# Host-laid parameters and gate weights, smaller first loads, gates one unit later, deferred rows of w_out, and a last product by token tiles

## The chip, the cores and the metric

One core of a Trainium2 chip runs the kernel. TensorE (PE) multiplies matrices, VectorE (DVE) and ScalarE (ACT) work on elements, GpSimd (POOL) does little here, and SyncE's queue (SP) issues DMA transfers. The metric is the device time of one execution in microseconds.

## The reference

One decoder layer for 2048 tokens of width 1024 in fp32:

```python
h = rmsnorm(x, norm_mix_g)
u = h @ w_in                       # 1024 x 3584, split into gate_b, gate_c, v, x_r, g
y_conv = gate_b * causal_dwconv(gate_c * v, conv_w)          # width 512, 3 taps
xr = causal_dwconv(x_r, rnn_conv_w) + rnn_conv_b             # width 1024, 4 taps
r = sigmoid(block_diag(xr, w_a) + b_a); i = sigmoid(block_diag(xr, w_x) + b_x)
a = exp(-8 * r * softplus(-lam)); bx = sqrt(1 - a*a) * (i * xr)
y_rnn = scan(a, bx) * gelu(g)
x = x + concat[rmsnorm(y_conv), rmsnorm(y_rnn)] @ w_out      # 1536 x 1024
h = rmsnorm(x, norm_mlp_g)
x = x + square(relu(h @ w_mlp_in)) @ w_mlp_out               # 1024 x 4096 x 1024
out = rmsnorm(x, final_norm_g)
```

## The kernel before

The tokens are cut into four blocks `b` of 512, and a block into four token tiles `t` of 128. Each fp32 operand is split into a rounded high part and the rest (`hi`, `lo`, type fp32r), and a product is the sum of three passes, hi·hi, lo·hi and hi·lo. ScalarE casts the high parts (line 174), VectorE subtracts for the low parts (line 175).

**Mixers.** `mixers(b, h)` goes through 14 units of 256 columns of `w_in` in the order x0 g0 x1 c0 g1 x2 v0 g2 x3 b0 g3 c1 v1 b1. Each unit is 48 products into one of four PSUM pairs. An x unit goes through `lru_conv` (empties PSUM, four taps on VectorE), `lru_split`, and then `lru_gates`, 12 small block-diagonal products per two column groups with sigmoids on ScalarE; `lru_scan` runs the recurrence on VectorE. Units c, v and b make the short convolution (`conv_c`, `conv_v`, `conv_b`). `part(n)` does pieces of the next block's row norm.

**Block 0's beginning** is written out by hand for ScalarE, VectorE and TensorE. The products of x0 and g0 (`start_x`, `start_g`) start from unnormalised x, loaded transposed; the row factors are computed beside them, spread over the partitions with a product of a diagonal matrix with ones (`spread`, `bc`, line 421) and kept in `row0`, by which VectorE multiplies each of block 0's units when it empties PSUM. The gain `norm_mix_g` and all small parameter vectors are loaded as rows and turned with transposes on TensorE. Two groups of small products with ones (`WARM`) run while the first loads are under way.

**Output projection.** `w_out_rows` multiplies the recurrent half in four row groups `pr` by four token tiles into `po[0..3]`, all four PSUM pairs at once; the fourth pair first serves the next block's spread and the sums for the norm (`stats`). `w_out_conv` adds the convolution's half, and the residual is kept.

**MLP.** Two blocks together form 2x2 block products with seven multiplications instead of eight (the `Up` and `Down` classes; ORDER is 1, 2, 6, 5, 7, 3, 4). In `Down`, product `i` is done in two halves `a`, each over four token tiles; after `a == 1`, `drain` adds PSUM to the residual. In the last quarter of the inner width product 3 completes block b and product 4 completes block b+1 in its first 512 columns. `finish(b)` squares, sums, takes the root, scales and stores each token tile.

Outside the hand-written stretches a scheduler orders each engine's instructions by the place in the program and its own model of time. Weights live in 15 slots (`wp`), other temporaries in 29 (`tp`); `take(name, ahead)` uses a unit's weights, loads those of later units and splits them.

Of the kernel before, what the change touches and what calls it, by code (L numbers as in the profile page):

```python
# [38 lines left out]
def KEEP(u, n):  # L39
# [3 lines left out]
ROWS = [  # L43
    ("conv_w", 12),
# [12 lines left out]
def block_kernel(  # L57
# [3 lines left out]
    norm_mix_g,  # L61
    w_in,
    conv_w,
    rnn_conv_w,
    rnn_conv_b,
    w_a,
    b_a,
    w_x,
    b_x,
    lru_lambda,  # L70
    g_norm_conv,
    g_norm_rnn,
# [5 lines left out]
    x_t,  # L78
    out,
# [184 lines left out]
    ones = cp.tile([P, P], F32, name="ones")  # L264
    nc.gpsimd.memset(ones, 1.0)
# [36 lines left out]
    def load_gates():  # L302

        r = temp("gate_raw", (P, NLRU, P))
        for e in range(2):
            for g, src in enumerate((w_a, w_x)):
                col = 64 * ((g + e) % 2)
                sv = src[0].rearrange("(c e) i j -> e i c j", e=2)
                nc.sync.dma_start(r[64 * e : 64 * e + 64, :, col : col + 64], sv[e])
        return r  # L310
# [9 lines left out]
    g_row = temp("g_row", (KD, P))  # L320

    def start_w(u, i):
# [3 lines left out]
    nc.sync.dma_start(g_row, norm_mix_g[0].rearrange("(k p) -> k p", p=P))  # L326
    load_xt(0, (0,))
    start_w(0, 0)
    load_xt(0, (1,))
    start_w(0, 1)  # L330
    load_xt(0, (2,))
    load_xt(0, (3,))
# [4 lines left out]
    nc.scalar.activation(warm, ones[:, 0:1], AF.Sqrt)  # L337
    nrows = sum(n for _, n in ROWS)
    prow = temp("prow", (P, P))
    srcs = dict(  # L340
        conv_w=conv_w[0].rearrange("k (c q) -> (k c) q", q=P),
        rnn_conv_w=rnn_conv_w[0].rearrange("k (c q) -> (k c) q", q=P),
        rnn_conv_b=rnn_conv_b.rearrange("o (c q) -> (o c) q", q=P),
        b_a=b_a.rearrange("o (c q) -> (o c) q", q=P),
        b_x=b_x.rearrange("o (c q) -> (o c) q", q=P),
        lru_lambda=lru_lambda.rearrange("o (c q) -> (o c) q", q=P),
        g_norm_conv=g_norm_conv.rearrange("o (c q) -> (o c) q", q=P),
        g_norm_rnn=g_norm_rnn.rearrange("o (c q) -> (o c) q", q=P),
    )
    off = {}  # L350
    o = 0
    for nm, n in ROWS:
        if nm == "b_x_swapped":
            for e in range(2):
                nc.sync.dma_start(
                    prow[o : o + n, 64 * e : 64 * e + 64],
                    srcs["b_x"][:, 64 - 64 * e : 128 - 64 * e],
                )
# [713 lines left out]
    def w_out_rows(b, ysB, accB, during):  # L1072
        po = [psum("po") for _ in range(NT)]
        for pr in range(4):
# [4 lines left out]
            if pr:  # L1079
                during(pr)  # L1080
# [263 lines left out]
```

## Time and profile before

| | us |
|---|---|
| median of three runs | 2173.37 (2171.5 to 2177.3) |
| profiled execution, own time | 2173.16 |
| its span, first to last instruction | 2171.4 |
| TensorE busy | 2152.1 |
| VectorE busy | 1471.3 |
| ScalarE busy | 983.1 |

The span is what the trace covers; the profiled execution's own time is 1.76 us more. The engines work side by side, so their busy times don't add up. A line such as `PE po L421 <- DVE u L730: 3.3, 1, 3.3` says that TensorE, at line 421, stood idle 3.3 us in total until VectorE's line 730 was done, once, and at longest 3.3 us. In a timeline a row begins with its start and its duration in us. In a table of windows, the columns behind the stretch are its length, the busy time and number of instructions of PE, PEld, DVE, ACT and POOL, the granted TensorE clock, the DMA share and GB/s.

### The profile page before, as it was taken

What the parts mean: (1) busy time and instruction counts of PE and PEld (TensorE: products, weight loads), DVE (VectorE), ACT (ScalarE), POOL (GpSimd) and SP (SyncE); (2) the same over time, 40 slices, a digit from 0 to 9 for tenths busy, and PEclk for the clock granted to TensorE, in tenths of its full rate; (3) what the DMA queues carried; (4) which work ended last, traced back from release to release, by engine and by line L of the source; (5) the groups of instructions that cost most, each with busy time, mean ns of one, the idle gap of its engine ahead of it and who ended that gap; (6) DMA issues with size and microseconds to landing.
All of it is one profiled execution on the core that took longest, in us unless ns stands there. A gap on an engine that the chain in (4) does not pass through costs nothing.

```text
span 2171.4 us, 25196 instructions
## 1 busy us (share of the span) xinstructions
PE 2152.1 (99%) x9634; PEld 1773.1 (82%) x9634; DVE 1471.3 (68%) x1763; ACT 983.1 (45%) x1300; POOL 43.5 (2%) x50
## 2 busy tenths in 40 slices
PE   9999999999999999999999999999999999999997
PEld 7887888888888888888888888888888888888886
DVE  6878636668666678778754653545886666887866
ACT  6784355436533343334445623562464333333343
POOL 0100000000000000000001000000000000000000
PEclk9999999999999999999999999999999999999999
DMA  7898875742453576444285657456335355854422
GB/s 266 301 334 289 332 281 194 277 140 93 154 189 117 184 305 247 152 153 153 103 313 203 244 211 271 177 197 247 107 125 195 117 187 201 328 175 155 136 97 78
DMA packets 177769, 435.82 MB, mean 201 GB/s; under 512 B 17809, under 2 KB 68081, under 8 KB 177649
## 3 DMA queue, kind: packets, MB, share of 16 engines
q1 hardware_dynamic: 177648, 434.22, 54.8%
q8 instruction: 76, 1.25, 0.2%
q14 instruction: 45, 0.36, 0.0%
HBM read 312.53 MB, written 121.63 MB: 200 GB/s over the span
## 4 chain that ended last, share of the span: by engine, by line
PE 91%; DVE 4%; DMA 2%; ACT 2%; issue 1%; SPq 0%; POOL 0%; DVEq 0%; ACTq 0%; POOLq 0%
PE up L811 28%; PE dn L929 27%; PE po L253 12%; PE ps_x L229 6%; PE ps_g L229 6%; PE ps_c L229 3%; PE ps_v L229 3%; PE ps_b L229 3%; PE psri L652 1%; DVE xr L617 1%; DMA raw<-in_w_in_dram 1%; PE tps L1098 1%; PE start_x L488 1%; DMA xT<-in_x_t_dram 1%; DVE x L973 0%
## 5 line engine op out<-in xcount | busy, mean ns | idle before, releaser
L811 PE MATMUL up<-H,w_hi 128*128 128x512 f32 x1792 | 552.1, 389 | 0.0
L811 PEld LDWEIGHTS up<-H,w_hi 128*128 128x128 f32 x1792 | 336.0, 188 | 69.7
L811 PE MATMUL up<-H,w_lo 128*128 128x512 f32 x896 | 348.6, 389 | 0.0
L929 PE MATMUL dn<-w_hi,z_hi 128*128 128x512 f32 x896 | 348.5, 389 | 0.0
L929 PE MATMUL dn<-w_lo,z_hi 128*128 128x512 f32 x896 | 348.5, 389 | 0.0
L929 PE MATMUL dn<-w_hi,z_lo 128*128 128x512 f32 x896 | 348.5, 389 | 0.0
L175 DVE TENSOR_TENSOR w_lo<-w,w_hi 128x1024 fp32r<-128x1024 f32 x156 | 190.7, 1223 | 129.0 <-PE dn L929 51.3
L174 ACT CAST z_hi<-z 128x1024 fp32r<-128x1024 f32 x112 | 118.2, 1056 | 353.2 <-PE dn L929 314.2
L174 ACT CAST w_hi<-w 128x1024 fp32r<-128x1024 f32 x156 | 163.8, 1050 | 250.0 <-PE up L811 123.3
L929 PEld LDWEIGHTS dn<-w_hi,z_lo 128*128 128x128 f32 x896 | 168.2, 188 | 35.1
L929 PEld LDWEIGHTS dn<-w_hi,z_hi 128*128 128x128 f32 x896 | 168.2, 188 | 34.9
L929 PEld LDWEIGHTS dn<-w_lo,z_hi 128*128 128x128 f32 x896 | 168.2, 188 | 34.8
L811 PEld LDWEIGHTS up<-H,w_lo 128*128 128x128 f32 x896 | 168.2, 188 | 34.8
L941 DVE TENSOR_TENSOR x<-dn,x 128x1024 f32<-128x1024 f32 x112 | 136.8, 1221 | 24.9 <-PE dn L929 23.5
L175 DVE TENSOR_TENSOR z_lo<-z,z_hi 128x1024 fp32r<-128x1024 f32 x112 | 136.6, 1219 | 15.1 <-ACT z_hi L174 15.1
L253 PE MATMUL po<-w_hi,y_hi 128*128 128x512 f32 x384 | 121.1, 397 | 0.0
L253 PE MATMUL po<-w_lo,y_hi 128*128 128x512 f32 x384 | 119.0, 390 | 0.0
L253 PE MATMUL po<-w_hi,y_lo 128*128 128x512 f32 x384 | 118.7, 390 | 0.0
L608 DVE TENSOR_SCALAR xr<-xr_in,prm 128x512 f32<-128x512 f32 x32 | 17.3, 550 | 115.3 <-ACT xr_in L601 115.2
L229 PE MATMUL ps_x<-h_hi,w_hi 128*128 128x512 f32 x240 | 93.5, 390 | 0.0
L229 PE MATMUL ps_g<-h_hi,w_hi 128*128 128x512 f32 x240 | 93.5, 390 | 0.0
L229 PE MATMUL ps_x<-h_lo,w_hi 128*128 128x512 f32 x240 | 93.4, 389 | 0.0
(234 smaller groups left out, 3469.6 us busy)
## 6 DMA issues: line engine op xcount, KB each, us to landing
w_hi<-d_w SPq DMA_DIRECT2D x114, 512.0 KB
w_lo<-d_w SPq DMA_DIRECT2D x114, 512.0 KB
z<-d_z SPq DMA_DIRECT2D x112, 512.0 KB
w<-in_w_mlp_in_dram SPq DMA_DIRECT2D x64, 512.0 KB
d_z<-snap SPq DMA_DIRECT2D x64, 512.0 KB
d_z<-z SPq DMA_DIRECT2D x48, 512.0 KB
w<-in_w_mlp_out_dram SPq DMA_DIRECT2D x48, 512.0 KB
d_w<-w_hi SPq DMA_DIRECT2D x40, 512.0 KB
```

What stands on the lines that cost most here:

```text
L174: nc.scalar.copy(hi, src)
L175: return (lo_engine or V).tensor_tensor(lo, src, hi.bitcast(F32), SUB).ins
L229: nc.tensor.matmul(ps[:, j, lo:hi], ws[k // 4][:, k % 4, j * P : (j + 1) * P], hs[:, k, lo:hi], start=k == 0 and i == 0, stop=k == KD - 1 ...
L253: nc.tensor.matmul(ps[:, half, :], ys[:, j, t * P : (t + 1) * P], ws[j][:, 0, half * 512 : (half + 1) * 512], start=first and i == 0, stop ...
L488: nc.tensor.matmul(start_x[:, j], w[a][k // 4][:, k % 4, j * P : (j + 1) * P], h[c][:, k], start=k == 0 and n == 0, stop=k == KD - 1 and n ...
L608: V.tensor_scalar(xr[:, j, :], xr_in[:, j, 0:TB], par("rnn_conv_w", c), par("rnn_conv_b", c), MUL, ADD,)
L617: V.scalar_tensor_tensor(xr[:, j, :], xr_in[:, j, k : k + TB], par("rnn_conv_w", 8 * k + c), xr[:, j, :], MUL, ADD,)
L652: nc.tensor.matmul(pr_[:, e, :], ws[own, c, :], xsrc[own, j, :], start=i == 0, stop=i == 2)
L811: nc.tensor.matmul(ps[:, j, :], ws[:, k, j * P : (j + 1) * P], hs(k), start=i in (1, 2, 5) and k == 0 and n == 0, stop=k == 3 and n == len ...
L929: nc.tensor.matmul(ps[t // 2][:, t % 2, :], zs[:, p, t * P : (t + 1) * P], ws[:, p, :], start=i in (1, 2, 5) and a == 0 and p == 0 and n == 0,
L941: V.tensor_add(xt[b, th, dh], ps[th], xt[b, th, dh])
L1098: nc.tensor.transpose(ps[:, k, :], xs[:, k // 4, k % 4 * P : (k % 4 + 1) * P], ident)
```

## The change

1. The host hands over `rows_t` (all parameter vectors, `norm_mix_g` among them, already turned to 128 partitions by 104 columns) and `gate_w` (the gate weights as the kernel keeps them). One transfer each takes the place of 11 row transfers with two transposes, and of four transfers.
2. The first loads are 256 KB instead of 512 KB, and the first two weight pieces are issued on ScalarE's queue. The casts of the first weights go in four pieces too.
3. x1 joins x0 and g0 in the hand-written beginning, and the spread comes in the middle of x1. `spread` becomes two fp32r products (high and low part of the diagonal) instead of one fp32 product. For block 0 the square of the row factor is kept as well, so that `conv_c` multiplies by the square and `conv_v` has one multiplication less; the remaining one moves from `conv_b` to the end of `conv_v`.
4. `lru_conv` is cut into `lru_take` (empties PSUM) and the taps, and each gate stage comes one unit later: behind c0, v0, b0 and c1 instead of x1, x2, x3 and g3. The split of the second y moves from `w_out_rows` to the end of `mixers`.
5. In `w_out_rows` the fourth token tile of row groups 0 and 1 is done after the other three tiles of both; `take` of group 1 looks one unit ahead instead of two.
6. In the last quarter of `Down`, product 4 is done with both halves for one token tile after the other, in the order 0, 2, 1, 3 (`multiply_last`), and each tile is added, squared, scaled and stored at once. The class `Finish` squares the 512 columns that are complete earlier, and multiplies them by the gain, under the products before; ScalarE scales these columns at the end.

```diff
+    nc.sync.dma_start(prm, rows_t)
+    for q in range(4):
+        r = temp("xT")
+        for i in range(2):
+            k0 = 256 * q + 128 * i
+            nc.sync.dma_start(r[:, i, :], x_t[k0 : k0 + P, 0:TB])
...
+        ks = slice(2 * (q % 2), 2 * (q % 2) + 2)
+        (nc.scalar if q < 2 else nc.sync).dma_start(
+            raws[0][q // 2][:, ks, :], units[0][1][0][q // 2][:, ks, :]
+        )
...
     def diagonal(rs, n):
-        diag = temp("diag", (P, n, P))
+        hi = temp("diag_hi", (P, n, P), F32R)
+        lo = temp("diag_lo", (P, n, P), F32R)
         for k in range(n):
-            V.tensor_scalar(diag[:, k, :], ident, rs[:, k : k + 1], None, MUL)
-        return diag
+            f = rs[:, k : k + 1]
+            V.tensor_scalar(hi[:, k, :], ident, f, None, MUL)
+            V.scalar_tensor_tensor(lo[:, k, :], ident, f, hi[:, k, :].bitcast(F32), MUL, SUB)
+        return hi, lo
...
         mm_cols(start_g, w, h, 0, ks=range(4, KD))
+        mm_cols(start_g, w, h, 1, ks=range(4, KD))
+        w = take("x1", ahead=0)
+        start_x1 = psum("start_x1")
+        mm_cols(start_x1, w, h, 0, ks=range(4))
+        mm_cols(start_x1, w, h, 1, ks=range(4))
         bc = spread(diag, NT)
...
+        mm_cols(start_x1, w, h, 0, ks=range(4, KD))
+        mm_cols(start_x1, w, h, 1, ks=range(4, KD))
+        nc.scalar.copy(row0[:, 0], bc)
+        nc.scalar.activation(row0[:, 1], bc, AF.Square)
...
         gs = lru_gelu(0, h, row)
-        psx = col_unit("x1", h)
+        x_in = lru_take(1, col_unit("x1", h), row)
+        gc = conv_c(0, h, row2)
+        part(0)
+        part(1)
         st = lru_gates(0, xr, xs, gs)
-        xr = lru_conv(1, psx, row)
+        xr = lru_conv(1, x_in)
...
+            w = take("oB%d" % pr, ahead=1 if pr == 1 else OUT_AHEAD)
...
             for t in range(NT):
+                if pr < 2 and t == 3:
+                    held.append((y, w))
+                    continue
                 for j in range(2):
                     mm_rows(po[t], y, w, j, t, pr == 0 and j == 0, pr == 3 and j == 1)
+            if pr == 1:
+                if b + 1 < NB:
+                    next_part(b + 1, 8, po[3][:, 0, :])
+                rB = stats(accB, D, "B", po[3][:, 1, 0:NT])
+                for n, (y, w) in enumerate(held):
+                    during(n)
+                    for j in range(2):
+                        mm_rows(po[3], y, w, j, 3, n == 0 and j == 0, False)
...
+            def take_tile(t, ps):
+                self.add(t, ps)
+                if t == 0:
+                    other.factors(0, NT)
+                if t in (0, 2):
+                    other.rows(t, 2)
+                if held:
+                    end(held.pop())
+                held.append(t)
+                if t == NT - 1:
+                    end(held.pop())
...
+                end = s == NS // 2 - 1
+                if not (end and i == 4):
+                    downs[s].multiply(i, a)
+                    if a == 1:
+                        downs[s].drain(i, b)
+                elif a == 1:
+                    downs[s].multiply_last(ends[1].tiles(ends[0]))
...
+                if end and (i, a) == (5, 0):
+                    ends = [Finish(b, 0), Finish(b + 1, 1)]
+                    ends[0].first()
+                if end and (i, a) == (3, 1):
+                    for t in range(NT):
+                        ends[0].add(t, None)
+                if end and (i, a) == (7, 1):
+                    ends[1].first()
```

More of the change, by code (lines that the diff above doesn't have):

```diff
@@ L1061, in mixers @@
         fold(accB)
-        part(3)
-        gc = conv_c(1, h, row)
-        part(4)
+        part(6)
         load_x(b)
```

303 lines of the change are left out of this document (170 added, 133 removed).

## The prediction

> **What bounds the kernel now.** I read the busy times first, then who waited for whom on TensorE, then the chain of waits, then the windows around each place where TensorE stands still.
>
> ```profile
> span 2171.4 us, 25196 instructions
> PE 2152.1 (99%) x9634; PEld 1773.1 (82%) x9634; DVE 1471.3 (68%) x1763; ACT 983.1 (45%) x1300; POOL 43.5 (2%) x50
> PE po L421 <- DVE u L730: 3.3, 1, 3.3
> PE start_x L488 <- ACT w_hi L472: 2.4, 1, 2.4
> 5.89 1.33 ACT h_hi L468 x2
> 7.24 1.05 ACT w_hi L472
> 8.33 12.60 PE start_x L488 x48
> 29.10 0.88 PE bc L421 x2
> 269.16 10.88 PE ps_x L229 x48
> 415.12 0.86 PE po L421 x2
> ```
>
> TensorE is busy 99% of the span. A unit of 48 products takes 10.88 us, 0.227 us each, whether it is x, g, c, v or b. So only three things can shorten this kernel: TensorE idling, TensorE at a lower clock, and products that are not needed. TensorE waits 2.4 us before its first real product and 3.3 us once in the first output projection; the rest of its idle time is the tail behind the last product. Nothing between 190 us and that tail is a stall, so whatever the change does there can only hold or lose.
>
> Everything is counted against the profiled execution: 2173.16 us, 1.76 above its span, and 0.21 below the median of 2173.37.
>
> **The start.** Loads land in the order issued, and a landing is seen about 1.1 us after the bytes have moved.
>
> ```profile
> 0.73 1.28 ACT L337 ACT_TABLE_LOAD   x1 [0.73 <-PEq L1330]
> 2.00:4.75 2.75, 2.75 (x14) 2.50 (x14) 0.17 (x1) 0.40 (x4) 0.00 (x0) 1.00 0.79 189
> 2.00:6.35 4.35, 3.95 (x23) 3.51 (x22) 0.17 (x1) 0.86 (x5) 0.00 (x0) 1.00 0.88 252
> 20.77 0.39 PE L229 MATMUL start_g<-h_hi,w_hi 128*128 128x512 f32 x1
> ```
>
> By 4.75 us 0.52 MB had moved (2.75 us at 189 GB/s): the first 512 KB block of x transposed, used from 5.89. By 6.35 it is 1.1 MB, which brings the first weight block, cast at 7.24. After, the first product wants the parameter table (53 KB), 256 KB of x and 256 KB of weights, 0.57 MB, the weights issued on ScalarE's queue. With two queues sharing the engines, part of the second x piece moves too: some 0.62 MB, there at 5.1 us, seen at 6.2. Then one cast of x (1.33/2 = 0.67) and one of half a weight block (0.53) put the first product at 7.4 instead of 8.33. If ScalarE's transfers stand behind its table load (1.28 us) the weights start later but x alone sooner; the same arithmetic gives 6.9 to 7.4. A quarter of `start_x` needs 1.9 us of ScalarE (two casts of x, one of weights), about 2.1 of VectorE and 12 products x 0.227 = 2.72 of TensorE, so TensorE then sets the pace, with about 0.3 us of waiting in the first quarter.
>
> `start_x` now runs from 8.33 to 20.77, 12.44 us instead of 10.88. The clock says why:
>
> ```profile
> 7.50:8.00 0.50, 0.00 (x0) 0.00 (x0) 0.50 (x1) 0.50 (x1) 0.00 (x0) 0.96 1.02 358
> 8.00:8.50 0.50, 0.17 (x1) 0.17 (x2) 0.25 (x2) 0.28 (x1) 0.00 (x0) 0.50 1.08 383
> 11.00:11.50 0.50, 0.50 (x3) 0.39 (x2) 0.49 (x1) 0.29 (x1) 0.00 (x0) 0.63 1.08 408
> 4.54:7.95 3.41, 1.41 (x12) 1.22 (x11) 1.30 (x2) 2.05 (x3) 0.00 (x0) 1.00 1.03 363
> ```
>
> The granted clock falls to 0.50 near 7.95 us and comes back near 11.3: 3.4 us at half speed, 1.7 us lost. In the 3.41 us before the fall TensorE was busy for 1.41. After, the warm-up products are as many and end at about the same time, 5.9, and the first real product comes 0.9 us earlier, so that stretch would be some 55% busy instead of 41%. The bounds are: clock kept (gain 0.9 + 1.7 - 0.3 = 2.3) and clock lost again (from 7.4 on, ending near 19.9: gain 0.9). The nearest row is the fall itself; I take 0.9. The Trainium skill ("TensorE: Matmul & The Clock Gate", section "The HAM clock gate") has the throttle decided in free-running windows of about 3.4 us, fully throttled after an idle one. The 3.4 us of half speed agree with the length; that a stretch 41% busy was enough to lose the clock is harsher than the page's idle window. By the page's wording a mostly busy window would keep the clock, and the start would gain 2.3.
>
> Behind it, `start_g` to the next unit takes 32.65 - 20.77 = 11.88 us:
>
> ```profile
> 32.65 0.39 PE L229 MATMUL ps_x<-h_hi,w_hi 128*128 128x512 f32 x1
> ```
>
> 1.0 of that is not products of the unit: the fp32 spread of row factors (0.88) and the transpose of the parameters. After, the transpose is gone and the spread is two fp32r products, 0.45. Gain 0.55. The third unit's weights, split in the prologue, cost 2 casts and 2 subtractions (about 1.05 and 1.22 each) on engines that have over 20 us for them.
>
> The same spread stands in three later output projections at 0.86: 3 x (0.86 - 0.45) = 1.2 gained, on TensorE's own path. The extra VectorE instructions for its low part (4 x about 0.25 us per block) lie beside products.
>
> **The stall in the first output projection.** For batch block 0:
>
> ```profile
> 170.45 0.61 PE L253 MATMUL po<-w_hi,y_hi 128*128 128x512 f32 x2
> 182.09 2.07 PE L421 MATMUL po<-diag,ones 128*128 128x512 f32 x2 [3.31 <-DVE u L730]
> 221.14 0.79 PE sps L582 x8
> 406.79 0.62 PE L253 MATMUL po<-w_hi,y_hi 128*128 128x512 f32 x2
> 452.64 0.79 PE sps L582 x8
> 182.00:183.00 1.00, 0.91 (x1) 0.50 (x2) 0.04 (x1) 0.93 (x1) 0.00 (x0) 0.52 0.09 37
> ```
>
> From the stage's first product to the statistics behind it: 50.69 us in block 0, 45.85 in block 1. The difference, 4.8 us, is 3.3 of stall and the rest a half clock after it. TensorE wants the fourth PSUM pair, still held by the last mixer unit until VectorE has multiplied it out (line 730). After, tokens 384 to 511 of the first two row groups come after the rest, so the fourth pair is wanted 36 products = 8.2 us later. Against that, VectorE's whole block-0 work starts later in TensorE's order: the spread comes after 48+48+24 products, not 48+36, again 36 products = 8.2 us. So the deferral alone would only pay back the later row factors. What must absorb the delay is VectorE's slack:
>
> ```profile
> 31.10:178.80 147.70, 147.68 (x668) 119.83 (x666) 124.38 (x157) 106.33 (x134) 14.70 (x10) 1.00 0.85 307
> L663 DVE TENSOR_TENSOR gi<-gi,xr 128x1024 f32<-128x1024 f32 x16 | 19.6, 1225 | 93.0 <-ACT gi L660 93.0
> L707 DVE TENSOR_TENSOR gc<-gc,row 128x1024 f32<-128x1024 f32 x2 | 2.4, 1222 | 0.0
> 171.26 1.22 DVE L708 TENSOR_TENSOR cv<-ps_v,gc 128x1024 f32<-128x1024 f32 x1
> ```
>
> VectorE is idle 147.7 - 124.4 = 23.3 us of this stretch. Over all 16 gate stages it waits 93.0 us for the sigmoids, 5.8 each, so 23 in one block: that is the slack. Gates one unit later put 10.9 us of other work in front of each such wait. The change also takes away two multiplications (2.4 us), and adds one split of y before the projection (1.5) and the low parts of the spread (1.0): nothing on balance. With 3.3 us wanted and up to 23 to draw on, I take the stall as gone: 4.8 gained. Bounds: 4.8, and a new stall at the third PSUM pair (rival 2).
>
> The gates' products themselves, 12 per pair, are unchanged. The first take of x now empties its PSUM buffer before the gates instead of after, which releases a buffer earlier. Moving the split of the second y into the mixers is covered by the same slack; in blocks 1 to 3 TensorE has no stall to lose.
>
> **The tail.**
>
> ```profile
> 2142.47 1.23 DVE L175 TENSOR_TENSOR w_lo<-w,w_hi 128x1024 fp32r<-128x1024 f32 x1 [1.95 <-PE dn L929]
> 2158.52 0.39 PE L929 MATMUL dn<-w_hi,z_lo 128*128 128x512 f32 x1
> 2159.30 1.21 DVE L941 TENSOR_TENSOR x<-dn,x 128x1024 f32<-128x1024 f32 x1
> 2160.23 0.61 ACT L965 ACTIVATE sq<-x 128x512 f32<-128x512 f32 x1
> 2160.43 0.15 DVE L371 RECIPROCAL rs_s<-rs_s 128x1 f32<-128x1 f32 x1
> 2161.06 0.16 DVE L378 TENSOR_TENSOR rs<-rs_s,rs_q 128x1 f32<-128x1 f32 x1
> 2159.30:2168.30 9.00, 0.00 (x0) 0.00 (x0) 8.89 (x32) 3.97 (x16) 0.00 (x0) 0.64 0.45 173
> 2168.35 0.33 SPq L974 DMA_DIRECT2D out_dram<-x  x1
> ```
>
> The last product M starts at 2158.52; the span ends at 2171.4, 12.88 later. For 9.0 us of that VectorE is 99% busy, on four token tiles at about 1.9 each (two multiplications of 0.66 and six short ones). After, tiles come out of the last product one by one, every 2.72 us, and only the last tile lies behind M. Its chain: add ready at M+0.78, 0.75 long; square and its sum 0.7; combination and root 0.45; reciprocal to factor 0.8; multiplication 0.75, ScalarE doing the other half beside it; two issues of 0.33: the last at M+4.7. From the last issue to the end it is 2171.4 - 2168.35 = 3.05 now: end at M+7.8. The other bound is VectorE's load: from the first tile (M-7.4) it has 4 adds (2.6), 8 multiplications (5.3), five factor chains (3.6), 11.5 us: until M+4.1. Both limits nearly meet, so I allow 0.4 for order: M+8.2, a gain of 4.7; ends 5.1 and, if the other half's four multiplications (2.7) end up before the last tile, 2.4. The earlier squares and gains of the finished halves are moved under the last seven products, where VectorE idles 1.95 us at a time and ScalarE is the less busy of the two. The second half's operands, now wanted at the start of the last product (2158.52 - 47 x 0.227 = 2147.9), are split by 2143.7.
>
> **Sum.** 0.9 + 0.55 + 1.2 + 4.8 + 4.7 = 12.15; 2173.16 - 12.15 = 2161.0 us.
>
> **Rivals.** (1) The clock is kept at the start: 1.4 more, 2159.6. For it: the gap shrinks from 2.4 to 1.5 us. Against it: the row of 41%. The page's rule above says the same.
> (2) VectorE's delay is not absorbed. Line 708 empties the third PSUM pair at 172.5 now, wanted at 170.45 + 24 x 0.227 = 175.9: 3.4 us to spare. 8.2 us later it is a stall of 4.8, with about 1.5 of slow clock: 2161.0 + 6.3 = 2167.3, no difference that counts. Against it: the 23 us of slack. Half absorbed, it costs about 1.
> (3) Slower: weights of the fourth row group come late. In block 1 they are issued as soon as the first group's buffers are free:
>
> ```profile
> 419.57 0.32 SPq L188 DMA_DIRECT2D w_lo<-d_w  x1
> 421.38 0.34 SPq L188 DMA_DIRECT2D w_hi<-d_w  x1
> 418.00:429.00 11.00, 11.00 (x49) 8.96 (x49) 3.64 (x12) 0.31 (x2) 0.00 (x0) 1.00 0.53 192
> ```
>
> Four transfers of 512 KB, wanted 21 us later. Deferral keeps the first group's buffers until the second group's end: issue near 428, wanted near 441, 13 us for 2 MB, or 160 GB/s. It decides below that rate. To be slower by over 0.3% three blocks must lose 12.15 + 6.5, 6.2 each: 4.6 of stall and the slow clock, transfers of 17.6 us or 119 GB/s. That window moved 192 with half of its DMA time unused: unlikely.
> (4) Small first loads move slowly. The window from 2 to 4.75 us, with 512 KB pieces, is at 189 GB/s only; were all 3.2 MB of the start to move at 240, they would end at 16.5 us and hold the last quarter of `start_x` by about 1.5 us: 2162.5. The Trainium skill ("DMA: Bandwidth & Descriptors", "Measured") wants transfers of 1 MiB and gives 138 GB/s for 64 KB and 341 for 1 MB, which speaks against the pieces. Here back-to-back 512 KB loads reach 383 to 408 in the rows above.
>
> **How the numbers follow.** Forecast 0.50, its own range 2158.5 to 2164; rival 1 0.20; rival 2 0.14, half of it beyond the bound; rival 3 0.04; rival 4 0.04; the rest, 0.08, is a tail or a start that gives less and small stalls elsewhere. 0.3% is 6.5 us, about what a measurement of this kernel can tell (its three runs spread over 5.8). Faster 0.82, same 0.12, slower 0.06. The range 2157 to 2167 holds the forecast, rivals 1 and 4 and most of 2.
>
> **What would show it.** First `start_x` product near 7.4, and its 48 products over 10.9 to 12.5 us, with the granted clock of 8 to 11 us deciding between forecast and rival 1. Spread as two products of 0.23. No wait of the spread in block 0 for line 730's successor, and a distance from the projection's first product to the statistics near 45 us. Last store issued under 5 us after the last product, end about 8 after it. A stall of TensorE on `po` in block 0, or on `w_hi`/`w_lo` in blocks 1 to 3, would prove the forecast wrong, as would VectorE still busy with the earlier half's rows when the last tile is ready.

## The result, and the profile after

The changed kernel took 2162.53 us (median of four runs, 2162.18 to 2162.96), beside 2175.12 for the kernel before in the same session (2171.5 to 2177.3): a ratio of 0.9946 (after over before), 95% interval 0.9933 to 0.996. The profiled execution took 2162.34 us with a span of 2160.5, against 2173.16 and 2171.4 before: 10.9 us of span. The forecast was 2161.0.

The busy times, TensorE's waits, and three rows of the chain of waits, of the kernel after:

```profile
span 2160.5 us, 25162 instructions
PE 2148.3 (99%) x9632; PEld 1772.2 (82%) x9632; DVE 1470.8 (68%) x1743; ACT 997.3 (46%) x1314; POOL 33.2 (2%) x50
PE po L245 <- DVE w_lo L167: 1.1, 1, 1.1
PE start_x L470 <- ACT w_hi L453: 0.7, 1, 0.7
7.34 11.35 PE start_x L470 x48
35.02 0.48 PE bc L403 x2
185.60 0.48 PE po L403 x2
```

The wait for line 730 is gone, and so is most of the wait before the first product. A new wait of 1.05 us (1.1 in the list) stands in the same output projection, for the low part of a block of `w_out` (line 167). The spread is two products in 0.48 us, where it was 0.86 to 0.88.

Milestones of TensorE from the two timelines (in which the statistics start 0.16 us sooner than in the chain), as the length of each stretch in us, and what it gained:

| stretch | before | after | gain | forecast |
|---|---|---|---|---|
| to the first real product | 8.33 | 7.34 | 0.99 | 0.9 |
| the 48 products of `start_x` | 12.44 | 11.19 | 1.25 | 0 |
| from there to the first `po` of block 0 | 149.68 | 149.22 | 0.46 | 0.55 |
| first `po` to the statistics, block 0 | 50.53 | 46.35 | 4.18 (0.41 of it the spread) | 4.8 + 0.4 |
| the statistics to the last product | 1937.54 | 1936.70 | 0.84 | 0.8 |
| the last product to the end | 12.88 | 9.70 | 3.18 | 4.7 |
| sum | 2171.4 | 2160.5 | 10.9 | 12.15 |

The windows of the kernel after that answer to those shown of before: the stretch in which the clock was lost before; VectorE over the mixers of block 0, over ten microseconds of the output projection, and behind the last product:

```profile
4.54:7.95 3.41, 2.69 (x12) 2.08 (x11) 1.33 (x2) 2.08 (x6) 0.00 (x0) 1.00 1.01 359
7.34:9.00 1.66, 1.66 (x6) 1.16 (x7) 1.66 (x4) 1.66 (x4) 0.00 (x0) 1.00 1.04 396
37.40:178.00 140.60, 140.48 (x636) 113.88 (x634) 121.03 (x159) 106.04 (x135) 10.23 (x10) 1.00 0.89 322
170.00:180.00 10.00, 8.95 (x40) 7.08 (x39) 10.00 (x12) 2.90 (x4) 1.69 (x1) 1.00 0.58 226
2150.80:2160.50 9.70, 0.39 (x2) 0.00 (x0) 4.45 (x18) 3.48 (x10) 0.00 (x0) 0.64 0.75 287
```

In the first row TensorE is busy 2.69 of 3.41 us, where it was 1.41 before, and the granted clock stays at 1.00 behind it. In the third VectorE is idle 19.6 us (140.6 less 121.0); before it was 23.3. In the fourth it has no idle time at all, and that is where TensorE waits 1.05 us for it. In the last VectorE has 4.45 us of work in 9.70, where it had 9.15 in 12.88, so VectorE no longer bounds the tail; what is left is one chain of dependent steps.

### The profile page after: what moved, and what is told of

Its sections match the earlier page's. It is cut to its first block, busy times and chain, and to the rows that moved or that the text cites. A ratio compares the mean times of both kernels' runs of the same rounds, so it can differ in the third digit from the quotient of the medians.

```text
span 2160.5 us, 25162 instructions
## 1 busy us (share of the span) xinstructions
PE 2148.3 (99%) x9632; PEld 1772.2 (82%) x9632; DVE 1470.8 (68%) x1743; ACT 997.3 (46%) x1314; POOL 33.2 (2%) x50
## 3 DMA queue, kind: packets, MB, share of 16 engines
q8 instruction: 76, 1.25, 0.2%
## 4 chain that ended last, share of the span: by engine, by line
PE 97%; DVE 1%; ACT 1%; issue 0%; DMA 0%; SPq 0%; ACTq 0%; DVEq 0%
PE up L801 28%; PE dn L919 27%; PE po L245 12%; PE ps_g L221 8%; PE ps_x L221 7%; PE ps_c L221 4%; PE ps_v L221 4%; PE ps_b L221 4%; PE psri L644 1%; PE tps L1186 1%; PE dn L938 1%; PE start_x L470 1%; PE start_x L221 1%; PE start_g L221 1%; DMA xT<-in_x_t_dram 0%
## 5 line engine op out<-in xcount | busy, mean ns | idle before, releaser
L919 PE MATMUL dn<-w_hi,z_hi 128*128 128x512 f32 x864 | 336.1, 389 | 0.0
L919 PE MATMUL dn<-w_lo,z_hi 128*128 128x512 f32 x864 | 336.1, 389 | 0.0
L919 PE MATMUL dn<-w_hi,z_lo 128*128 128x512 f32 x864 | 336.1, 389 | 0.0
L919 PEld LDWEIGHTS dn<-w_hi,z_hi 128*128 128x128 f32 x864 | 162.2, 188 | 33.8
L919 PEld LDWEIGHTS dn<-w_lo,z_hi 128*128 128x128 f32 x864 | 162.2, 188 | 33.6
L919 PEld LDWEIGHTS dn<-w_hi,z_lo 128*128 128x128 f32 x864 | 162.2, 188 | 33.5
L951 DVE TENSOR_TENSOR x<-dn,x 128x1024 f32<-128x1024 f32 x108 | 131.6, 1219 | 28.2 <-PE dn L919 28.0
L655 DVE TENSOR_TENSOR gi<-gi,xr 128x1024 f32<-128x1024 f32 x16 | 19.6, 1224 | 113.1 <-ACT gi L652 113.1
L221 PE MATMUL ps_g<-h_lo,w_hi 128*128 128x512 f32 x240 | 93.5, 390 | 0.0
L221 PE MATMUL ps_g<-h_hi,w_lo 128*128 128x512 f32 x240 | 93.4, 389 | 0.0
```

The costliest lines, as they stand in the source:

```text
L221: nc.tensor.matmul(ps[:, j, lo:hi], ws[k // 4][:, k % 4, j * P : (j + 1) * P], hs[:, k, lo:hi], start=k == 0 and i == 0, stop=k == KD - 1 ...
L655: V.tensor_mul(gi, gi, xr)
L919: nc.tensor.matmul(ps[t // 2][:, t % 2, :], zs[:, p, t * P : (t + 1) * P], ws[:, p, :], start=i in (1, 2, 5) and a == 0 and p == 0 and n == 0,
L951: V.tensor_add(xt[b, th, dh], ps[th], xt[b, th, dh])
```

## Undoing one part at a time

Each of these four kernels is the changed one with one part put back. They ran on one chip, where the kernel before took 2172.71 us. The changed kernel as it is was not run there; it took 2162.53 us in the first measurement and, below, 2163.81 on another chip, so differences of about 1 us in the times say little, and the stages of the traces are read instead. "Stage" is the distance from the first `po` to the statistics in block 0, 46.35 us in the kernel after.

**The tail.** Product 4 is again done in two halves and `finish` follows it:

```diff
-                if not (end and i == 4):
-                    downs[s].multiply(i, a)
-                    if a == 1:
-                        downs[s].drain(i, b)
-                elif a == 1:
-                    downs[s].multiply_last(ends[1].tiles(ends[0]))
+                downs[s].multiply(i, a)
+                if a == 1:
+                    downs[s].drain(i, b)
```

> The changed kernel with its old tail: product 4 in two halves, each over all token tiles, and the old finish. Theory, by the two traces: the tail from the last product's start to the end goes from 9.70 back to 12.88 us, so the time rises by 3.2 us (median 2162.5 to 2165.7) and nothing else moves. Rival: the early squares and gains under the products cost something elsewhere, or helped elsewhere, and the rise is below 2 or above 5 us.

Measured: 2166.32 us (2165.65 to 2167.24), span 2164.6. From the last product to the end it is 12.92 us again, 3.22 more than 9.70, and VectorE is again the bound there:

```profile
2151.68:2161.50 9.82, 0.38 (x2) 0.00 (x0) 9.15 (x33) 4.74 (x18) 0.00 (x0) 0.63 0.43 166
```

So the tail's part is worth 3.2 us against this profile, and not the 4.7 of the forecast. In eight profiles of kernels that keep the changed tail, the end comes 8.85 to 9.81 us behind the last product, which makes it 3.1 to 4.1.

**The deferral.** `w_out_rows`, and the place of the second y's split, as before:

```diff
-                if pr < 2 and t == 3:
-                    held.append((y, w))
-                    continue
...
-            w = take("oB%d" % pr, ahead=1 if pr == 1 else OUT_AHEAD)
+            w = take("oB%d" % pr, ahead=OUT_AHEAD)
```

> The changed kernel with the old row order in the first half of w_out: no deferral, the split of the second y back in its old place, two units ahead. Theory (VectorE's later start was absorbed only in part, and the deferral hides the rest): in the changed kernel line 720 ends at 180.0 us while the fourth PSUM pair would be wanted at 167.75 + 8.17 = 175.9, so TensorE stands still about 4 us in block 0 and runs slowly for about 3.4 behind it: 5 to 6 us more, 2167.5 to 2168.5. Rival (the slack had absorbed the delay, as forecast): no stall to bring back, the time stays at 2162.5 or falls by the 1.05 us of the new wait.

Measured: 2174.78 us (2172.59 to 2178.65), ratio to before 1.0012 (1.0002 to 1.0021): eleven to twelve microseconds lost, twice what was expected. TensorE's waits:

```profile
PE po L245 <- DVE ys_B L578: 3.5, 2, 2.1
PE po L403 <- DVE u L720: 2.8, 1, 2.8
PE po L570 <- ACT bcs L1082: 1.5, 1, 1.5
```

Block 0's stage takes 51.40 us, 5.05 more: the wait for the last unit (now line 720), and behind it 6.8 us at a granted clock of 0.50. That is the 5 to 6 of the expectation. The rest, 9.53 us, lies behind the statistics of block 0: in each of the three later output projections TensorE waits once (1.50 us at 416.56 for the spread's copy, 1.46 at 1261.67 and 2.09 at 1495.25 for `ys_B`), the first two times with a stretch of slow clock behind it. The kernel before had none of these waits, and the kernel after has none. So with the other parts of the change in place every block needs this part, not block 0 alone. A wait on `w_lo` is not in the list: without the deferral the 1.05 us of the kernel after are not there. That the later gates open these waits is likely, since they move VectorE's and ScalarE's work towards the projection in every block, but both parts were not undone together.

**The later gates.** Each gate stage in its old place, one unit earlier:

```diff
-        x_in = lru_take(1, col_unit("x1", h), row)
-        gc = conv_c(0, h, row2)
+        psx = col_unit("x1", h)
         st = lru_gates(0, xr, xs, gs)
-        xr = lru_conv(1, x_in)
+        xr = lru_conv(1, lru_take(1, psx, row))
```

> The changed kernel with the gates back in their old places (behind x1, x2, x3 and g3); x1 stays in the hand-written beginning, the deferral stays. Theory of the forecast: gates one unit later are what gives VectorE other work before its waits for the sigmoids; without it those waits in block 0 grow and TensorE stalls more than the 1.05 us of now, at the gates or in w_out: 2 to 6 us more. Rival (by the page the waits for the sigmoids rose from 93.0 to 113.1 us, so later gates did not shorten them): the waits fall back towards 93 us and the time is the same within 1 us, or lower by the 1.05 us.

Measured: 2171.85 us (2169.82 to 2173.27), ratio 0.9993 (0.9983 to 1.0002): 8.0 to 9.3 us lost, more than expected, and at another place:

```profile
PE psri L644 <- ACT gate_hi L166: 4.8, 1, 4.8
40.92:45.68 4.76, 0.00 (x0) 0.00 (x1) 4.76 (x6) 2.14 (x4) 0.91 (x1) 0.90 1.04 421
45.68:49.00 3.32, 3.19 (x12) 1.67 (x12) 3.32 (x6) 2.87 (x4) 0.21 (x1) 0.50 1.02 417
```

The first row is a wait, the two others are windows. x1 is now in the written-out beginning, so in the old order the first gates come directly after it, and nothing is left for TensorE to do while VectorE makes the taps of x0 and ScalarE casts the gate weights. It stands 4.76 us and then runs some 6 us at about half speed; from the first `start_g` to the first `po` 156.98 us pass instead of 149.22, 7.76 more. A second wait, 1.84 us for a high part of y, stands at 223.92, behind the statistics. The forecast had seen the later gates as slack for VectorE. By this trace, what they are needed for first is to make x1's early place possible at all. The first half of the rival came as well: VectorE's waits for the sigmoids are 93.6 us here, as in the kernel before (93.0), and 113.1 in the kernel after. The later gates made these waits longer, not shorter.

**The smaller first loads.**

```diff
-    for q in range(4):
-        r = temp("xT")
-        for i in range(2):
...
+    load_xt(0, (0,))
+    start_w(0, 0)
+    load_xt(0, (1,))
+    start_w(0, 1)
+    load_xt(0, (2,))
+    load_xt(0, (3,))
```

> The changed kernel with the first loads whole again: 512 KB each, all on SyncE's queue; the casts stay in pieces. Theory of the forecast (bytes): the first x block is seen at 5.9 us as before, the first weights at 7.2 us, then a cast of 0.6: first product near 7.85 instead of 7.34, with the clock lost or kept by chance: 0.5 to 2.2 us more. Rival (the first x piece of 256 KB was seen at 5.87 us, as the 512 KB block before, so pieces gave nothing and the smaller casts gave all): first product within 0.2 us of 7.34 and the same time.

Measured: 2164.01 us (2161.92 to 2166.16), span 2162.4. The first product starts at 8.07 us, 0.73 later than with the small pieces, and the clock is lost (windows):

```profile
9.00:10.00 1.00, 1.00 (x5) 0.77 (x4) 0.93 (x2) 1.00 (x3) 0.00 (x0) 0.80 1.08 412
10.00:12.00 2.00, 2.00 (x7) 1.52 (x6) 1.52 (x3) 1.26 (x3) 0.00 (x0) 0.50 1.05 399
```

In ten profiles of kernels that have the small pieces and the same beginning, the first product comes at 7.13 to 7.75 us, so the pieces and their second queue bring 0.3 to 0.9 us. The rest of what this kernel lost in its profile (`start_x` 12.82 us instead of 11.19) is the clock. In time it can't be told from the changed kernel: 2164.01 us lies beside 2162.53 and 2163.81, and the fastest of its runs, 2161.92, is no slower than either. That the clock was kept in that execution is likely, but was not looked at.

## The clock at the start

Two kernels change only how many warm-up products run: 9 of each kind in the kernel before, 3 in the kernel after. They and the next two ran on another chip, where the kernel before took 2172.0 us.

```diff
-WARM = 6
+WARM = 9
```

> The kernel before with 18 warm-up products instead of 12 and nothing else: the idle stretch ahead of the first real product shrinks from 2.4 to about 0.7 us. Theory (the gap alone costs the clock, 1.7 us): start_x takes about 11 us instead of 12.4, the granted clock stays at 1.00 there, 1.3 to 1.7 us less than the kernel before, and the runs lie closer together. Rival (the clock is lost for another reason, or the loss is hidden by late loads): no gain, within 0.5 us.

> The changed kernel with 6 warm-up products instead of 12: they end near 4 us and TensorE idles some 3 us before its first product at 7.3. Theory (the changed kernel keeps its clock only because its gap is short): granted clock 0.50 for about 3.4 us, start_x near 12.5 to 13 us instead of 11.2, 1.5 to 2 us more: 2164 to 2164.5. Rival (short warm-up is enough, or pieces make the start bound by loads): the same time within 0.4 us.

With 9 in the kernel before, the wait ahead of the first product shrinks from 2.38 to 0.41 us, the clock is kept and `start_x` takes 11.20 us in the chain: 1.4 gained there, as expected. Yet the time is 2174.56 us (2169.81 to 2176.03), ratio 1.0007 (0.9998 to 1.0017). The windows of the output projection of block 0 say where it went, for this kernel and, in the third row, the kernel before:

```profile
176.95:180.04 3.09, 0.48 (x3) 0.06 (x1) 2.99 (x4) 0.00 (x0) 0.00 (x0) 1.00 0.85 339
180.04:190.30 10.26, 9.55 (x24) 7.00 (x25) 6.69 (x11) 8.35 (x13) 0.00 (x0) 0.50 0.03 14
182.00:185.45 3.45, 3.36 (x6) 1.87 (x7) 2.33 (x4) 3.38 (x6) 0.00 (x0) 0.51 0.03 11
```

The stall is the same 3.3 us, but the half clock behind it lasts 10.26 us instead of 3.45: three times the 3.41 us of a window instead of once. From the first `po` to the statistics 53.42 us pass instead of 50.53: 2.9 us more, which takes back more than the start had gained. The same stall is thus worth about 5 to 8 us. Why the clock came back after one window in the one kernel and after three in the other, the runs do not show. The 17 runs of the kernel before on that chip, 2169.8 to 2177.1 us, would fit such steps; their traces were not looked at.

With 3 in the kernel after, 2164.14 us (2163.85 to 2164.61), span 2162.8: TensorE idles 3.43 us, and `start_x` takes 13.47 us, 2.28 more than 11.19. The time is the expected one, the stretch is longer than the 12.5 to 13 us expected. The timeline shows half speed where the column of the granted clock, for which 0.50 was expected, does not: it reads 1.00 over all of it.

```profile
7.49 2.08 PE L470 MATMUL start_x<-h_hi,w_hi 128*128 128x512 f32 x4 [3.43 <-ACT w_hi L453]
9.37 1.91 PE L470 MATMUL start_x<-h_lo,w_hi 128*128 128x512 f32 x4
13.69 1.09 PE L470 MATMUL start_x<-h_lo,w_hi 128*128 128x512 f32 x4
```

Four products take 1.9 to 2.1 us and later 1.09; the first twelve take 5.27 us, from 7.49 to 12.76.

## What is left: two tries that failed, and two by their place

**The spread a quarter of x1 earlier**, so that VectorE gets the row factors sooner and the last wait of 1.05 us goes:

```diff
         start_x1 = psum("start_x1")
         mm_cols(start_x1, w, h, 0, ks=range(4))
+        bc = spread(diag, NT)
         mm_cols(start_x1, w, h, 1, ks=range(4))
-        bc = spread(diag, NT)
```

> The changed kernel with the spread of block 0's row factors 12 products (2.7 us) earlier, a quarter into x1 instead of half; the diagonal is ready at 30.4 us, the new place comes at about 32.1. Theory (VectorE begins block 0 too late in TensorE's order, and that is what leaves the 1.05 us wait for the second row group's low parts): the wait goes, 1.0 us less, and the distance from w_out's first product to the statistics falls from 46.5 to 45.4. Rival (VectorE's order and its waits for the sigmoids set the moment, not its beginning): wait and time unchanged within 0.3 us.

Measured: 2168.1 us (2167.24 to 2169.93), span 2165.5. The spread runs at 32.23 instead of 35.02, and the wait grows to 5.48 us. Rows of this kernel, TensorE's, VectorE's and SyncE's:

```profile
181.93 1.22 PE L245 MATMUL po<-w_lo,y_hi 128*128 128x512 f32 x2 [5.48 <-DVE w_lo L167]
179.52 1.22 DVE L714 TENSOR_TENSOR u<-u,row 128x1024 f32<-128x1024 f32 x1
180.66 2.35 DVE L167 TENSOR_TENSOR w_lo<-raw,w_hi 128x1024 fp32r<-128x1024 f32 x2
126.57 10.40 SPq L148 DMA_DIRECT2D d_w<-w_hi  x2
137.54 1.85 SPq L161 DMA_DIRECT2D raw<-in_w_out_dram  x2
```

and of the kernel after:

```profile
175.27 1.21 DVE L714 TENSOR_TENSOR u<-u,row 128x1024 f32<-128x1024 f32 x1
177.67 1.21 DVE L167 TENSOR_TENSOR w_lo<-raw,w_hi 128x1024 fp32r<-128x1024 f32 x1
124.57 0.33 SPq L161 DMA_DIRECT2D raw<-in_w_out_dram  x1
```

The scheduler, given the spread earlier, wrote other orders. On SyncE's queue two stores of weights stand for 10.4 us ahead of the first load of `w_out`, which goes out at 137.54 instead of 124.57; on VectorE, which has no gap here in either kernel, both low parts of the second row group are left to 180.66, where the kernel after had one left, at 177.67. So earlier row factors alone do not remove this wait: line 714 itself comes 4.25 us later here. The first of the two low parts had been cast at 167.6 and then waited 13 us in VectorE's order, which by then also held those of the first row group (161.93 and 166.12, in the kernel after 146.48 and 149.87). Which of the two reorderings did it was not tried, nor the earlier spread with the order of the kernel after.

**The other half's rows first in the tail, none held back**, so that the last tile finds ScalarE free:

```diff
-                if t in (0, 2):
-                    other.rows(t, 2)
-                if held:
-                    end(held.pop())
-                held.append(t)
-                if t == NT - 1:
-                    end(held.pop())
+                self.factors(t, 1)
+                self.rows(t, 1)
...
+                    ends[0].factors(0, NT)
+                    ends[0].rows(0, NT)
```

> The changed kernel with another order in the tail: the finished block's factors, rows and stores come ahead of product 4's tiles, and each tile of product 4 is scaled and stored at once instead of one tile later. Theory (the forecast tail of 8.2 us became 9.7 because earlier tiles' rows stood ahead of the last tile's factors on ScalarE and VectorE, and because six stores came within 3 us): last product to end 8.2 to 8.7, 1.0 to 1.5 us less time. Rival (the chain itself or the store is longer than summed): 9.4 or more, time unchanged within 0.3 us.

Measured: 2165.39 us (2163.25 to 2167.61), span 2161.7. From the last product to the end 8.93 us, 0.77 less, and the last issue comes 4.57 us behind that product instead of 5.47; but the products themselves now wait:

```profile
2150.12 0.50 PE L938 MATMUL dn<-w_hi,z_hi 128*128 128x512 f32 x1 [1.30 <-DVE x L993]
```

Four multiplications stand on VectorE ahead of the addition that empties the PSUM pair, and from the statistics to the last product 1938.55 us pass instead of 1936.70. Holding rows back is what keeps the last products running.

The last four kernels ran on a third chip of these experiments, where the kernel before took 2172.07 us. The first is the changed kernel, once more.

> The changed kernel itself once more, beside the three runs below on the same chip, so that each is compared with it there. Expected: 2162 to 2163 us, as before (2162.18 to 2162.96). If this chip's runs are slower than that by a whole multiple of about 1.7 us, the clock's windows fall differently against the same gaps, and the differences below are to be read against this run and not against 2162.5.

Measured: 2163.81 us (2162.77 to 2165.26), ratio 0.9957 (0.9943 to 0.997), span 2162.2. All stretches behind the start agree with the first profile within 0.06 us. The start doesn't: the first product comes at 7.75 and `start_x` takes 12.49 us. The second twelve warm-up products, first here, then in the first profile, and the window behind:

```profile
3.85 1.63 PE L442 MATMUL start_x<-ones_raw 128*128 128x128 f32 x12
3.86 2.77 PE L442 MATMUL start_x<-ones_raw 128*128 128x128 f32 x12
7.75:9.00 1.25, 1.25 (x3) 1.03 (x4) 1.25 (x3) 1.25 (x3) 0.00 (x0) 0.50 1.05 397
```

Here the clock came up in the middle of the warm-up, so the same products were done 1.15 us sooner, the gap behind them was 2.26 us instead of 0.71, and the clock fell again. Of the program nothing differs. So the start's gain is 2.24 us in the one profile and 0.53 in the other, and the forecast (0.9) and rival 1 (2.3) both came about, in different executions. They are not equally frequent. Eight more profiles show this beginning, in kernels changed only behind it: in all of them `start_x` takes 11.18 to 11.22 us and the start gains 1.9 to 2.5 us. In the fourteen profiles of this study half clock came behind an idle time of 1.61, 2.26, 2.38 and 3.43 us ahead of the first product, and did not come behind ten between 0.41 and 1.57. The length alone does not decide, though: in the output projections, half clock came behind a wait of 1.46 us (the kernel without the deferral, at 1261.67) and not behind one of 2.09 (the same kernel, at 1495.25). The Trainium skill ("TensorE: Matmul & The Clock Gate", "What's actually happening") says that the window runs free of the kernel's start, so that the place of the change depends on the phase; the two warm-up rows above agree with it. The same section has the clock fall after an idle window; here it fell after less, with TensorE busy 1.41 of 3.41 us before the change, so for this case the measurement decides.

**The low parts of the second row group on GpSimd** (block 0 alone):

```diff
-            split_into(hi, lo, r, lo_engine)
+            split_into(hi, lo, r, nc.gpsimd if units[u][0] == "oB1" and u < NU else lo_engine)
```

> The changed kernel with one edit: in block 0 the low parts of the second w_out row group (two subtractions of 128x1024, 1.13 us each on VectorE) are made by GpSimd. Theory: the 1.05 us that is left of the block-0 wait is VectorE's saturation (it is busy 10.00 of the 10 us from 170 to 180, GpSimd 1.69), so taking 2.27 us off VectorE there removes that wait: span 1.05 us shorter, 2161.5 us. Rival one: GpSimd makes a low part in well over 1.13 us, so the second one arrives later than VectorE's did and the wait grows; at 2.5 us each from the landing of the rows it still fits, since the rows had landed before 170. Rival two: a low part of y or the product of ps_b (line 720) is next in line and takes the wait's place at once: less than 0.3 us gained.

Measured: 2164.12 us (2163.95 to 2167.13), span 2162.2; the stage takes 47.42 us, 1.07 longer. The wait for `w_lo` is gone, and two for a low part of y (0.50 and 0.72) and one for a `ys_B` (0.3) came. GpSimd's row and VectorE's beside it:

```profile
160.14 5.31 POOL L167 TENSOR_TENSOR w_lo<-raw,w_hi 128x1024 fp32r<-128x1024 f32 x2 [12.20 <-DMA x<-in_x_dram]
160.29 1.22 DVE L698 TENSOR_TENSOR cv<-ps_v,gc 128x1024 f32<-128x1024 f32 x1
161.42 1.77 DVE L670 TENSOR_SCALAR r<-v 128x1024 f32<-128x1024 f32 x1
163.12 2.88 DVE L551 SCALAR_TENSOR_TENSOR y_lo<-s,prm,y_hi 128x512 fp32r<-128x512 f32 x1
```

In the kernel after, the two last take 0.68 and 0.74 us. So VectorE was relieved of 2.27 us and lost 1.09 + 2.14 = 3.2. The multiplication that reads PSUM (line 698) lost nothing. Each of the other two ended 0.4 to 0.6 us behind the end of a GpSimd instruction (two of 2.65 us from 160.14 on, to 162.8 and 165.45), which looks like waiting, not like sharing. The Trainium skill ("SBUF — State Buffer", "SBUF: two separate sides") has it so: GpSimd and VectorE lock one pair of ports for whole instructions, against VectorE's two-port modes and its instructions with two SBUF inputs. The trace agrees: both instructions that lost time end behind one of GpSimd's, and line 698, with one of its two inputs in PSUM, took its 1.22 us. Rival two of the expectation had named a low part of y as the next in line; that VectorE itself would lose time, no part of the expectation had.

**The order on ScalarE in the last 8 us**, and one store from another queue:

```diff
-                nc.sync.dma_start(outf[r0 : r0 + P, HALF[self.dh]], xv)
+                (queue or nc.sync).dma_start(outf[r0 : r0 + P, HALF[self.dh]], xv)
...
+                if t == NT - 1:
+                    for k in (held[0], t):
+                        self.factors(k, 1)
+                    with tc.issue_after(self.root): self.rows(held.pop(), 1)
+                    self.rows(t, 1, nc.scalar)
+                elif held: end(held.pop())
+                held.append(t)
```

> The changed kernel with the order on ScalarE changed in the last 8 us: the square root of the last token tile goes ahead of the scaling of the tile before it (0.71 us), and the last tile's first half is stored from ScalarE's queue instead of SyncE's. All other engines keep their order. Theory: the last store's issue ends the kernel 4.23 us later, and it was held by the square root (2154.04, though its operand was there at 2153.41) and by one more issue ahead of it (0.43 us). Expected: last issue 0.6 to 1.0 us nearer to the last product (5.47 us now), last product to end 9.70 to about 8.9, time 2161.6 to 2161.9 us. Rival: what ends the kernel is the landing of the stores that queue on the DMA rings (4.23 us behind the last issue against 3.05 in the kernel before): then an earlier issue only waits longer, and the time stays within 0.2 us.

Measured: 2161.52 us (2161.20 to 2162.11), ratio 0.9946 (0.9934 to 0.9959), span 2159.5; from the last product to the end 8.72 us. The root, and SyncE's last issue, of the kernel after and then of this one:

```profile
2152.72 1.42 ACT L1026 ACTIVATE x<-x,fs_r 128x512 f32<-128x512 f32 x2
2154.04 0.19 ACT L1010 ACTIVATE rs_s<-rs_a 128x1 f32<-128x1 f32 x1
2156.27 0.41 SPq L1030 DMA_DIRECT2D out_dram<-x  x1
2153.47 0.20 ACT L1010 ACTIVATE rs_s<-rs_a 128x1 f32<-128x1 f32 x1
2155.67 0.33 SPq L1030 DMA_DIRECT2D out_dram<-x  x1
```

With the last products at 2150.80 and 2150.78, the last issue came at 5.47 us behind them and now at 4.89: 0.58 gained, the lower edge of what was expected. The remaining 0.4 is the landing, 4.23 us from that issue to the end and now 3.83. It is not the edit's for certain: in the eight profiles with the changed tail as it was, the last issue stands 5.46 to 5.48 us behind the last product each time, but from there to the end 3.39 to 4.34 us pass. Against the kernel after on the same chip the median is 2.3 us lower. In the two profiles it is 2.7 us of span, of which 1.7 are the clock at the start, where the two programs are the same, and 0.96 the tail.

**Both edits.**

> Both edits, of pool_lo and of tail_v2. They are 1970 us apart in the span, so the gains should add: 1.6 to 2.0 us under the changed kernel, 2160.5 to 2160.9 us, last product at about 2149.75 and span about 2158.8. If a gain shows in one of them alone and not here, the clock's windows after the changed gap are the first suspect.

Measured: 2163.28 us (2162.72 to 2164.11), span 2161.7. The expected 2160.5 to 2160.9 did not come. The tail keeps its gain (8.73 us); the stage in block 0 takes 48.00 us, 1.65 more than in the kernel after. So the tail's edit alone is the fastest kernel of this study, 10.6 us under the kernel before on its chip, and under the changed one by a profiled 0.6 to 1.0.

## Why the forecast came near, and where its steps were off

- **Start** (0.9 forecast, 2.24 in the first profile, 0.53 in one other). The first product at 7.4 held (7.34, and 7.13 to 7.75 over the ten profiles of this beginning). What failed is the choice between the two bounds. It rested on a warm-up that ends "at about the same time, 5.9"; it ended at 5.48 to 6.63, as the clock came up, and the gap behind it was 0.63 to 2.26 us. In nine of the ten profiles the clock was kept. So rival 1, which had a chance of 0.20, is what usually happens, and the forecast's case came once. Of the kernel before only one profile was read, with the clock lost.
- **Prologue** (0.55; 0.46) and **three later spreads** (1.2; 0.84 for the two behind block 0's stage, and the forecast's 0.41 set down for the one in it): as worked out. The product pair costs 0.48 and not 0.45.
- **The stall in block 0** (4.8; 3.77 without the spread). The stall on PSUM and its slow clock went, as forecast, but 1.05 us of waiting came for a low part of weights (0.9 to 1.5 in six profiles of kernels whose edits lie elsewhere). Four rows of the kernel after, of VectorE and TensorE:

```profile
160.07 1.22 DVE L698 TENSOR_TENSOR cv<-ps_v,gc 128x1024 f32<-128x1024 f32 x1
178.80 1.21 DVE L720 TENSOR_TENSOR u<-ps_b,u 128x1024 f32<-128x1024 f32 x1
178.93 0.73 PE L245 MATMUL po<-w_lo,y_hi 128*128 128x512 f32 x2 [1.05 <-DVE w_lo L167]
185.44 0.40 PE L403 MATMUL po<-diag_hi,ones_r 128*128 128x512 f32 x1
```

  The cover was there. VectorE's first work on x0 comes 8.9 us later than before, measured from the first `po` (the forecast had 8.2), but line 720, which frees the fourth pair, only 0.7 us later than line 730 had: it ends 12.3 us behind the first `po`, where line 730 had ended 11.6 behind it. TensorE came to the pair 5.4 us later still. The step that failed is where the cover comes from. Of the 8.3 us absorbed, VectorE's idle time gave 3.86 (23.43 us before, 19.57 after), and 4.47 are less work ahead of that line (127.51 us before, 123.04 after; two low parts of the third row group, 2.4 us, now come behind it). The waits for the sigmoids, which the forecast called the slack, gave nothing. It took a quarter of the 93.0 us of all 16, 23 us, for block 0; the trace has 11.9 us there before, and 15.1 after. Over the whole kernel they grew too:

```profile
L655 DVE TENSOR_TENSOR gi<-gi,xr 128x1024 f32<-128x1024 f32 x16 | 19.6, 1224 | 113.1 <-ACT gi L652 113.1
```

  What the forecast left out is the order of the weights. With the fourth token tile held back, TensorE comes to the second row group 36 products behind its first and not 48, 2.7 us sooner. The second low part of that group had its cast by ScalarE (line 166, at 160.98) ready at 162.0 and stood in VectorE's order at 177.67. That this order makes the wait is read from these rows and not tried by itself: in the kernel without the deferral the wait is absent, but there TensorE had stood still for 2.8 us just before. What kept the larger stall away was the deferral, as its undoing shows (5.05 us in this stage). Rival 2 did not come: the third PSUM pair, by line 698, was free at 161.3, 11 us sooner than before (172.5), and not 8.2 later. That rival 2, half absorbed, was priced at about 1 us, and that 1.05 us came, is chance.
- **The tail** (4.7; 3.18, and 3.22 by undoing it). The forecast had the last issue at M+4.7 (M is the start of the last product) and the landing at 3.05 us. They were 5.47 and 4.23. Of the first, 0.58 are the root behind a scaling on ScalarE and one issue more ahead of the last, by the experiment with the order on ScalarE. The second was read from a tail whose stores had been spread over 9 us; six of the stores now leave in the last 3 us. With the old tail three profiles have 3.0 to 3.1 us there, with the new one eight have 3.39 to 4.34. That the landing is longer because of the stores' crowding was not tried.
- **Rivals 3 and 4**: no TensorE wait on weights in blocks 1 to 3, and 394 to 397 GB/s from 7.5 to 11.5 us, while small pieces move; neither came.
- The sum, 10.9 for 12.15 us, is near partly by luck: the start's surplus of 1.3 us hid about half of what the tail and block 0 fell short by. In the one profile without that surplus the kernel's span is 1.7 us longer.

That the parts depend on each other the forecast did not say: undone one by one, tail, deferral and gates lose 3.8, 12.3 and 9.3 us of median against the first measurement (1.3 less each against the other chip's), together about twice the whole gain. The host-laid parameters and the new spread were not undone by themselves; their 0.46 and 0.84 us are read from the two profiles.

## What to carry to other kernels

When work is put earlier on the bounding engine, ask which later stage loses its cover: the parts of such a change are to be priced together, and each undone by itself. When an order is changed to want one thing later, look at what it wants sooner. A stall's price is its length and, behind all of the longest and some of the shorter ones here, one or more clock windows at half speed, so a stall that is only moved can change price; and a warm-up measured once shows one execution, so look at several. The idle time of an engine is not slack as a sum: look at what ends each wait, in the stage in question and not as an average over all. Here the waits for the sigmoids gave nothing, and the other idle time did.

## What the runs showed of the hardware

- A stretch of 3.4 us with TensorE busy for 41% was followed by half clock. In the output projections half clock followed none of the waits up to 1.37 us, two of five between 1.46 and 2.09 us, and all four of 2.8 us and more. The half clock came in stretches of 3.45, 6.8 and 10.26 us behind stalls of about 3 us in one and the same place.
- During the warm-up, and in the first 5.3 us of `start_x` in the kernel with the short one, products run at half speed while the column of the granted clock reads 1.00; the mean time of a product is the safer sign.
- A subtraction of 128x1024 takes GpSimd 2.65 us (VectorE 1.13), and two VectorE instructions beside it took 1.77 and 2.88 us instead of 0.68 and 0.74.
- From SyncE's last issue to the end 3.39 to 4.34 us passed in eight profiles with the same tail program, and 3.0 to 3.1 in three with the old one.
